# The first load of an RMSNorm-GELU kernel, split by rows over both DMA queues, with two of the last stores merged

## Chip, cores, metric

One core of one Trainium2 chip. The metric is the device time of one execution in microseconds, median of several runs; the profile's span is some 1.8 us shorter, because it starts and ends inside the execution.

## The reference

```python
# x: (8, 1024, 2048) float32, gamma: (2048,), eps: 1e-5
rms = np.sqrt(np.mean(x ** 2, axis=-1, keepdims=True) + eps)
out = gamma * x / rms
return 0.5 * out * (1 + np.tanh(np.sqrt(2 / np.pi) * (out + 0.044715 * out ** 3)))
```

8,192 rows of 8 KB are read once and written once: 67.1 MB each way.

## The kernel before

The rows are cut into 16 groups. A group is 128 partitions of 4 rows each (32 KB in one piece per partition, 4 MB in all), and six slots in SBUF hold groups. SyncE issues the loads, ScalarE issues gamma and the stores, each on its own DMA queue (q1 is SyncE's, q10 is ScalarE's). Per group, ScalarE squares and sums four rows, GpSimd makes 1/rms, VectorE multiplies by gamma (which TensorE has spread over the partitions in PSUM), ScalarE does Gelu and issues the store. A slot is loaded again when its store has landed.

```python
P = 128; ROWS = 4; SLOTS = 6; NARROW = 128
# ...
whole = [(R, [(0, R * D)])]
store_pieces = {
    0: [(R, [(0, NARROW), (NARROW, R * D)])],
    G - 1: [(1, [(r * D, r * D + D)]) for r in range(R)],
}
def load(g):
    nc.sync.dma_start(out=slot[g % SLOTS], in_=x3[g])
# ... squares, scale, inverse_rms cut ...
def gelu_store(g):
    # ... per entry (n, stores): Gelu on n rows, then
            for a, b in stores:
                nc.scalar.dma_start(out=dst[:, a:b], in_=flat[:, a:b])

for k in range(0, D, CHUNK):                      # four gamma pieces of 2 KB
    nc.scalar.dma_start(out=gamma_row[...], in_=gamma[k : k + CHUNK]...)
for g in range(SLOTS):
    load(g)
# ... memsets, warm-up, the matmuls that spread gamma ...
for g in range(G + 1):
    if g < G:
        squares(g); inverse_rms(g); scale(g)
    if g:
        gelu_store(g - 1)
        if g - 1 + SLOTS < G:
            load(g - 1 + SLOTS)
```

Of the kernel before, what the change touches and what calls it, by code (L numbers as in the profile page):

```python
# [1 line left out]

# [4 lines left out]

FP32 = mybir.dt.float32
ALU = mybir.AluOpType
ACT = mybir.ActivationFunctionType  # L10

P = 128
ROWS = 4
SLOTS = 6

GW = 32
CHUNK = 512

NARROW = 128


@with_exitstack
def kernel(
    ctx: ExitStack,
    tc: tile.TileContext,
    x: bass.AP,
    gamma: bass.AP,
    eps: bass.AP,
    out: bass.AP,
):  # L30




    nc = tc.nc
    D = x.shape[-1]
    R = ROWS
    eps_f = float(eps)
    x3 = x.rearrange("b s d -> (b s) d").rearrange("(g p r) d -> g p r d", p=P, r=R)
    o3 = out.rearrange("b s d -> (b s) d").rearrange("(g p r) d -> g p r d", p=P, r=R)  # L40
    G = x3.shape[0]

    sbuf = ctx.enter_context(tc.tile_pool(name="sbuf", bufs=1))
    psum = ctx.enter_context(
        tc.tile_pool(name="psum", bufs=1, space=bass.MemoryType.PSUM)
    )
    slot = [sbuf.tile([P, R, D], FP32, name=f"slot{i}") for i in range(SLOTS)]
    gamma_row = sbuf.tile([1, D // GW, GW + 4], FP32, name="gamma_row")
    ones = sbuf.tile([1, P], FP32, name="ones")
    warm = sbuf.tile([1, 1], FP32, name="warm")  # L50
    power = sbuf.tile([P, R], FP32, name="power")
    ssq = sbuf.tile([P, G, R], FP32, name="ssq")
    rstd = sbuf.tile([P, G, R], FP32, name="rstd")
    ms = sbuf.tile([P, R], FP32, name="ms")
    y = sbuf.tile([P, R], FP32, name="y")
    z = sbuf.tile([P, R], FP32, name="z")
    gamma_ps = psum.tile([P, D], FP32, name="gamma_ps")
    junk = psum.tile([P, D], FP32, name="junk")


    whole = [(R, [(0, R * D)])]
    store_pieces = {
        0: [(R, [(0, NARROW), (NARROW, R * D)])],
        G - 1: [(1, [(r * D, r * D + D)]) for r in range(R)],
    }
    scale_pieces = {G - 1: [(0, 1), (1, 1), (2, 1), (3, 1)]}

    def load(g):
        nc.sync.dma_start(out=slot[g % SLOTS], in_=x3[g])  # L69

    def squares(g):
        for r in range(R):
            nc.scalar.activation(  # L73
                out=junk,
                in_=slot[g % SLOTS][:, r, :],
                func=ACT.Square,
                accum_out=ssq[:, g, r : r + 1],
            )

    def scale(g):  # L80
        for r, n in scale_pieces.get(g, [(0, R)]):
            rows = slot[g % SLOTS][:, r : r + n, :]
            nc.vector.tensor_tensor(  # L83
                out=rows,
                in0=rows,
                in1=gamma_ps.unsqueeze(1).to_broadcast([P, n, D]),
                op=ALU.mult,
            )

    def inverse_rms(g):  # L90

        v = nc.gpsimd
        v.tensor_scalar(  # L93
            out=ms, in0=ssq[:, g, :], scalar1=1.0 / D, scalar2=eps_f,
            op0=ALU.mult, op1=ALU.add,
        )
        v.tensor_tensor(out=y, in0=ms, in1=power, op=ALU.pow)  # L97
        v.tensor_tensor(out=z, in0=y, in1=y, op=ALU.mult)  # L98
        v.tensor_tensor(out=z, in0=z, in1=ms, op=ALU.mult)  # L99
        v.tensor_scalar(  # L100
            out=z, in0=z, scalar1=-0.5, scalar2=1.5, op0=ALU.mult, op1=ALU.add
        )
        v.tensor_tensor(out=rstd[:, g, :], in0=z, in1=y, op=ALU.mult)  # L103

    def gelu_store(g):
        flat = slot[g % SLOTS].rearrange("p r d -> p (r d)")
        dst = o3[g].rearrange("p r d -> p (r d)")
        row = 0
        for n, stores in store_pieces.get(g, whole):
            for r in range(row, row + n):  # L110
                nc.scalar.activation(  # L111
                    out=slot[g % SLOTS][:, r, :],
                    in_=slot[g % SLOTS][:, r, :],
                    func=ACT.Gelu_apprx_tanh,
                    scale=rstd[:, g, r : r + 1],
                )
            row += n
            for a, b in stores:
                nc.scalar.dma_start(out=dst[:, a:b], in_=flat[:, a:b])  # L119

    with tc.manual_schedule():
        for k in range(0, D, CHUNK):
            nc.scalar.dma_start(
                out=gamma_row[:, k // GW : (k + CHUNK) // GW, 0:GW],
                in_=gamma[k : k + CHUNK].rearrange("(o a b) -> o a b", o=1, b=GW),
            )
        for g in range(SLOTS):
            load(g)
        nc.gpsimd.memset(power, -0.5)  # L129
        nc.vector.memset(warm, 0.0)  # L130
        nc.vector.memset(ones, 1.0)  # L131
        nc.scalar.activation(out=warm, in_=warm, func=ACT.Gelu_apprx_tanh)  # L132
        for k in range(0, D, CHUNK):
            nc.tensor.matmul(  # L134
                out=gamma_ps[:, k : k + CHUNK],
                lhsT=ones,
                rhs=gamma_row[:, k // GW : (k + CHUNK) // GW, 0:GW],
                start=True,
                stop=True,
            )  # L140
        for g in range(G + 1):
            if g < G:
                squares(g)
                inverse_rms(g)
                scale(g)
# [6 lines that stand above are left out]
# [1 line left out]
_INS = ['x', 'gamma', 'eps']  # L153
_OUTS = [((8, 1024, 2048), 'float32')]

_NUMBERS = {'eps': 9.999999747378752e-06}


# [26 lines left out]
```

## Time and profile before

| | before |
|---|---|
| time | 317.27 us (317.25 to 317.39, 4 runs) |
| span | 315.5 us |
| ScalarE, VectorE busy | 80%, 44% |
| DMA engines, both queues | 99.1% of 16 engines' span |
| mean rate | 426 GB/s |

From the table of DMA issues (count, size of one, median us from issue to landing):

```profile
slot<-in_x_dram SPq DMA_DIRECT2D x16, 4096.0 KB, 29.9
out_dram<-slot ACTq DMA_DIRECT2D x14, 4096.0 KB, 43.3
gamma_row<-in_gamma_dram ACTq DMA_DIRECT2D x4, 2.0 KB, 10.3
```

A 4 MB transfer alone would take about 10 us (4.19 MB at 430 GB/s). That loads take 30 us and stores 43 us from issue to landing says that both queues are long: the transfers are what everything else waits for.

The end of the chain of waits (start, length, what):

```profile
242.11 29.47 DMA slot<-in_x_dram
271.61 2.01 ACT junk L73 x2
...
287.31 0.34 ACTq L119
```

The last load lands at 271.6 us. From there to the end of the span, 44 us, only stores move, and ScalarE finishes the last group beside them by 297 us.

### The profile page before, as it was taken

To read this page: it belongs to the slowest core of one execution; us is meant where nothing else is said; L and a number is where in the kernel's file an instruction comes from. 1 tells how busy PE (TensorE), PEld (TensorE's weight loads), DVE (VectorE), ACT (ScalarE), POOL (GpSimd) and SP (SyncE) were. 2 spreads that over 40 slices of the span, in tenths; PEclk is the share of its full clock that TensorE was granted. 3 is DMA by queue.
4 is the path that set the end of the run, shared out by engine and by line. 5 is a ranking of instruction groups with operands and counts; after the bars stand their busy time and mean duration, and the time that the engine had idled before them with its cause. 6 is when DMAs were issued, how large, how long until landed. Compare 5 with 4: busy or idle time off the path is not lost.

```text
span 315.5 us, 479 instructions
## 1 busy us (share of the span) xinstructions
PE 7.9 (3%) x8; PEld 2.1 (1%) x8; DVE 139.4 (44%) x21; ACT 251.2 (80%) x194; POOL 32.3 (10%) x101
## 2 busy tenths in 40 slices
PE   0810000000000000000000000000000000000000
PEld 0200000000000000000000000000000000000000
DVE  0028909091918282827328082370824609480000
ACT  1289999999999999989596895969959599598500
POOL 0020202020202020202020020200202002020000
DMA  8999999999999999999999999999999999999997
GB/s 329 404 461 403 459 413 396 453 406 462 403 461 407 457 407 458 411 453 416 449 428 440 432 432 432 432 440 424 446 416 453 411 453 411 453 415 449 416 418 314
DMA packets 5315, 134.25 MB, mean 426 GB/s; under 512 B 704, under 2 KB 832, under 8 KB 832
## 3 DMA queue, kind: packets, MB, share of 16 engines
q1 hardware_dynamic: 2304, 67.11, 49.7%
q10 hardware_dynamic: 3008, 67.12, 49.4%
q14 instruction: 3, 0.02, 0.0%
HBM read 67.12 MB, written 67.11 MB: 425 GB/s over the span
## 4 chain that ended last, share of the span: by engine, by line
ACT 38%; DMA 32%; another core or an unknown queue 18%; issue 5%; ACTq 1%; SPq 0%
ACT slot L111 21%; DMA slot<-in_x_dram 16%; ACT junk L73 16%; DMA out_dram<-slot 15%; ACTq L119 1%; SPq L69 0%; ACTq L111 0%; ACTq L73 0%
## 5 line engine op out<-in xcount | busy, mean ns | idle before, releaser
L83 DVE TENSOR_TENSOR slot<-slot,gamma_ps 128x8192 f32<-128x8192 f32 (+1 forms) x19 | 139.2, 7338 | 142.3 <-ACT junk L73 142.3
L73 ACT ACTIVATE junk<-slot 128x2048 f32<-128x2048 f32 x64 | 120.4, 1881 | 40.8 <-DMA slot<-in_x_dram 36.8
L111 ACT ACTIVATE slot<-slot,rstd 128x2048 f32<-128x2048 f32 x64 | 123.0, 1987 | 1.7 <-ACT slot L111 1.7
L93 POOL TENSOR_SCALAR ms<-ssq 128x4 f32<-128x4 f32 x16 | 3.1, 194 | 242.8 <-ACT junk L73 242.8
L97 POOL TENSOR_TENSOR y<-ms,power 128x4 f32<-128x4 f32 x16 | 16.1, 1009 | 1.3
L73 ACT ACTIVATION_READ_ACCUMULATOR junk<-slot 128x1 f32 x64 | 11.9, 186 | 0.0
L134 PE MATMUL gamma_ps<-gamma_row,ones 1*128 1x512 f32 x8 | 7.9, 1112 | 9.2 <-DMA gamma_row<-in_gamma_dram 9.2
L132 ACT ACT_TABLE_LOAD x1 | 1.3, 1283 | 3.3 <-issue 3.3
L99 POOL TENSOR_TENSOR z<-z,ms 128x4 f32<-128x4 f32 x16 | 3.2, 201 | 1.3
L103 POOL TENSOR_TENSOR rstd<-z,y 128x4 f32<-128x4 f32 x16 | 3.2, 200 | 1.3
L98 POOL TENSOR_TENSOR z<-y 128x4 f32<-128x4 f32 x16 | 3.2, 200 | 1.3
L100 POOL TENSOR_SCALAR z<-z 128x4 f32<-128x4 f32 x16 | 3.1, 195 | 1.4
L134 PEld LDWEIGHTS gamma_ps<-gamma_row,ones 1*128 1x128 f32 x8 | 2.1, 306 | 13.4 <-issue 8.7
L130 DVE MEMSET warm<- 1x1 f32 x1 | 0.1, 59 | 0.8 <-PEq L166 0.8
L132 ACT ACTIVATE warm<-warm 1x1 f32<-1x1 f32 x1 | 0.2, 203 | 0.0
L131 DVE MEMSET ones<- 1x128 f32 x1 | 0.2, 165 | 0.0
L129 POOL MEMSET power<- 128x4 f32 x1 | 0.1, 102 | 0.3 <-POOLq L166 0.3
L166 POOL MEMSET const-float32-0.0<- 128x1 f32 x1 | 0.1, 99 | 0.2 <-issue 0.2
L166 POOL MEMSET const-bfloat16-1.0<- 128x1 bf16 x1 | 0.1, 102 | 0.0
L166 POOL MEMSET const-uint8-127<- 128x1 uint8 x1 | 0.1, 102 | 0.0
L166 POOL MEMSET const-float32-1.0<- 128x1 f32 x1 | 0.1, 99 | 0.0
## 6 DMA issues: line engine op xcount, KB each, us to landing
slot<-in_x_dram SPq DMA_DIRECT2D x16, 4096.0 KB, 29.9
out_dram<-slot ACTq DMA_DIRECT2D x14, 4096.0 KB, 43.3
out_dram<-slot ACTq DMA_DIRECT2D x4, 1024.0 KB, 17.5
out_dram<-slot ACTq DMA_DIRECT2D x1, 4032.0 KB, 28.5
gamma_row<-in_gamma_dram ACTq DMA_DIRECT2D x4, 2.0 KB, 10.3
out_dram<-slot ACTq DMA_DIRECT2D x1, 64.0 KB, 14.4
```

The costliest lines, as they stand in the source:

```text
L73: nc.scalar.activation(out=junk, in_=slot[g % SLOTS][:, r, :], func=ACT.Square, accum_out=ssq[:, g, r : r + 1],)
L83: nc.vector.tensor_tensor(out=rows, in0=rows, in1=gamma_ps.unsqueeze(1).to_broadcast([P, n, D]), op=ALU.mult,)
L93: v.tensor_scalar(out=ms, in0=ssq[:, g, :], scalar1=1.0 / D, scalar2=eps_f, op0=ALU.mult, op1=ALU.add,)
L97: v.tensor_tensor(out=y, in0=ms, in1=power, op=ALU.pow)
L98: v.tensor_tensor(out=z, in0=y, in1=y, op=ALU.mult)
L99: v.tensor_tensor(out=z, in0=z, in1=ms, op=ALU.mult)
L100: v.tensor_scalar(out=z, in0=z, scalar1=-0.5, scalar2=1.5, op0=ALU.mult, op1=ALU.add)
L103: v.tensor_tensor(out=rstd[:, g, :], in0=z, in1=y, op=ALU.mult)
L111: nc.scalar.activation(out=slot[g % SLOTS][:, r, :], in_=slot[g % SLOTS][:, r, :], func=ACT.Gelu_apprx_tanh, scale=rstd[:, g, r : r + 1],)
L119: nc.scalar.dma_start(out=dst[:, a:b], in_=flat[:, a:b])
L132: nc.scalar.activation(out=warm, in_=warm, func=ACT.Gelu_apprx_tanh)
L134: nc.tensor.matmul(out=gamma_ps[:, k : k + CHUNK], lhsT=ones, rhs=gamma_row[:, k // GW : (k + CHUNK) // GW, 0:GW], start=True, stop=True,)
```

## The change

The intent: ScalarE stands idle until load 0 has landed. Half of its rows per partition now come over each queue, both issued at once. The diff also merges the stores of rows 0 and 1 of the last group into one.

```diff
-        G - 1: [(1, [(r * D, r * D + D)]) for r in range(R)],
+        G - 1: [(2, [(0, 2 * D)])] + [(1, [(r * D, r * D + D)]) for r in (2, 3)],
...
     with tc.manual_schedule():
+        nc.sync.dma_start(out=slot[0][:, 0 : R // 2], in_=x3[0, :, 0 : R // 2])
+        nc.scalar.dma_start(out=slot[0][:, R // 2 :], in_=x3[0, :, R // 2 :])
         for k in range(0, D, CHUNK):
             nc.scalar.dma_start(
... gamma as before ...
-        for g in range(SLOTS):
+        for g in range(1, SLOTS):
             load(g)
```

## The prediction

> **What bounds the kernel now.** I read the page first: engine shares, the DMA row, the queues. Then I cut the span into stretches, and last looked at the start, because the change is there.
>
> The page, kernel before (the third column of a queue line is its share of 16 DMA engines' span):
>
> ```profile
> PE 7.9 (3%) x8; PEld 2.1 (1%) x8; DVE 139.4 (44%) x21; ACT 251.2 (80%) x194; POOL 32.3 (10%) x101
> DMA  8999999999999999999999999999999999999997
> DMA packets 5315, 134.25 MB, mean 426 GB/s; under 512 B 704, under 2 KB 832, under 8 KB 832
> q1 hardware_dynamic: 2304, 67.11, 49.7%
> q10 hardware_dynamic: 3008, 67.12, 49.4%
> HBM read 67.12 MB, written 67.11 MB: 425 GB/s over the span
> ```
>
> The busiest compute engine, ScalarE, is at 80%. The DMA engines are at nine tenths or more in 38 of 40 slices, and the two queues' shares add up to 99.1% of all 16 engines for the whole span. So bytes bound this kernel: 67.1 MB in, 67.1 MB out, none of it removable. The packets of q1, the load queue: 16 loads of 128 rows of 32 KB are 2048, and 16 completions on each of 16 engines are the other 256, tiny ones. One 32 KB packet takes 0.497 x 16 x 315.5 / 2048 = 1.225 us on its engine, or 16 x 32,768 B / 1.225 us = 428 GB/s for all 16.
>
> The same by stretches (the last two columns are the DMA engines' mean busy share and GB/s):
>
> ```profile
> 1.50:6.00 4.50, 0.00 (x0) 0.00 (x0) 0.00 (x0) 1.49 (x2) 0.00 (x0) 1.00 0.97 350
> 6.00:14.00 8.00, 4.82 (x5) 1.49 (x6) 0.00 (x0) 0.53 (x1) 0.00 (x0) 1.00 1.07 456
> 14.00:30.00 16.00, 3.07 (x4) 0.61 (x2) 8.40 (x1) 14.33 (x15) 2.01 (x6) 1.00 0.99 428
> 30.00:50.00 20.00, 0.00 (x0) 0.00 (x0) 11.69 (x3) 19.49 (x16) 4.00 (x12) 1.00 1.01 421
> 132.00:272.00 140.00, 0.00 (x0) 0.00 (x0) 65.22 (x8) 112.70 (x87) 13.98 (x42) 1.00 1.00 432
> 300.00:312.00 12.00, 0.00 (x0) 0.00 (x0) 0.00 (x0) 0.00 (x0) 0.00 (x0) 1.00 0.97 412
> 312.00:314.00 2.00, 0.00 (x0) 0.00 (x0) 0.00 (x0) 0.00 (x0) 0.00 (x0) 1.00 0.70 295
> ```
>
> The reader is to see that the DMA share is about 1.00 from 1.5 us until 312 us. Loads alone (14 to 30 us) run at 428 GB/s, loads with stores (132 to 272) at 432: one queue already fills the engines. The only place where a full share moves few bytes is the first: 350 GB/s in 1.5 to 6 us, although the share is 0.97. By the packet records the first packet on each engine takes some 2 us and every later one 1.213. That costs 4.5 x (432 - 350) / 432 = 0.85 us. Between 30 and 50 us, 20 x 11 / 432 = 0.5 us is lost. Nothing moves before about 1.7 us and after about 314 us.
>
> The start in order of time, and two waits of SyncE's queue:
>
> ```profile
> 13.47 1.88 ACT L73 ACTIVATE junk<-slot 128x2048 f32<-128x2048 f32 x1 [8.70 <-DMA slot<-in_x_dram]
> 21.60 8.69 DVE L83 TENSOR_TENSOR slot<-slot,gamma_ps 128x8192 f32<-128x8192 f32 x1 [20.60 <-ACT junk L73]
> 23.06 1.88 ACT L73 ACTIVATE junk<-slot 128x2048 f32<-128x2048 f32 x1 [1.49 <-DMA slot<-in_x_dram]
> ```
>
> ```profile
> SPq L69 <- DMA out_dram<-slot: 224.3, 10, 53.7
> SPq L69 <- DMA gamma_row<-in_gamma_dram: 10.2, 2, 7.9
> ```
>
> ScalarE waits 8.70 us for the first load, the squares of group 0 end at 21.6, and it waits again, 1.49 us, for load 1. This is the idleness that the change aims at. But SyncE itself waits 224.3 us in all for stores to land before it may reuse a slot: compute is ahead of the transfers nearly everywhere.
>
> **What the Trainium skill says.** "DMA: Bandwidth & Descriptors", section "Issuing engines are not separate DMA queues", says that DMAs run on the same 16 DMA engines whichever engine issued them and that several issuers only save issue time. The trace agrees so far as it can: one queue alone gives 428 GB/s, two give 432. Section "Queues, rings and completion order" says that each DMA engine takes turns among its rings packet by packet. The packet records agree: in the start each tiny gamma packet lies between two 32 KB load packets, 1.21 us apart. "Specifications" of that page puts the fabric ceiling at 435 GB/s; 432 here is 99% of it. "Perfetto Trace Analysis", section "DMA Optimizations", says that splitting helps if DMA engines are generally idle; here they are not.
>
> **The change part by part.** (1) Load 0 becomes two DMAs with 16 KB per partition. Bytes are equal; packets go from 128 of 32 KB to 256 of 16 KB. The packet records have 309 ns for an 8 KB store packet and 1213 for 32 KB; a straight line through them has 7.7 ns per packet besides the bytes. So 128 more packets and 16 more completions of 9 ns cost (128 x 7.7 + 16 x 9) / 16 = 0.07 us.
>
> (2) The diff also merges the stores of rows 0 and 1 of the last group: 128 packets and 16 completions fewer, minus 0.07 us. It delays that first piece by one row of Gelu, about 2.4 us (289.80 to 292.22 in the chain of waits). But the last piece is issued at 297.05 and takes 17.6 us to land, and every earlier one takes 17.5: there is a store backlog of 17 us, so a piece 2.4 us later costs nothing. Sum of (1) and (2): zero.
>
> (3) When does load 0 land? It lands now 12.7 us after issue, with the engines busy all that time; the same 4.19 MB can't land sooner on the same engines. If both halves share turns from the start, both land near 12.5 us. If ScalarE's ring is seen later, as with gamma (issued at 0.72, first packets near 6.1 us), SyncE's half lands near 8 to 10 us, and the other half takes turns with the 32 KB packets of load 1: it would land at 14 to 17 us. The built program shows that the squares of rows 0 and 1 wait for SyncE's half alone, so ScalarE can start two rows early and then wait. Squares 0 end between 20.5 and 25 instead of 21.6.
>
> (4) The gamma pieces now queue behind a half load on ScalarE's ring. Each takes two turns of 1.21 us beside load packets, so four take up to 9.7 us more, and gamma lands at 20 to 27 us instead of 14.5 (landings now: 7.5 to 11.9 us after issue). With the matmuls some 2 us after, VectorE starts on group 0 between 22 and 29 us instead of 21.6, and the first large store, now issued at 38.77, comes 0 to 7 us later. That is off the path: the six loads alone are 25.2 MB, 58 us at 430 GB/s, so the engines have load packets until about 60 us without any store, and then stores that have been waiting.
>
> (5) The built program shows different semaphore reuse at SyncE: load 3 now waits for ScalarE's half, load 4 for load 1 (it waited for a gamma piece, the 10.2 us line). Load 3 then goes out near 13 to 17 us, load 4 near 23 us. At each moment at least one full load of 9.7 us still stands in the queue, so the ring doesn't run dry. The waits of later stores on earlier ones keep their pattern.
>
> Sum: +0.07 - 0.07, plus whatever the 0.85 us of the first packets becomes. I give two rings some chance to overlap part of it, -0.1 us on average. 317.28 - 0.1 is 317.2.
>
> **The rivals.** A, the intended one: ScalarE begins 3 to 5 us earlier and the whole kernel shifts by it, to about 313. For it speaks the 8.70 us wait; against it that compute is ahead already (224.3 us of SyncE's waits are for stores) and that the bytes would have to move at 134.25 MB / (313 - 1.8 - 1.7 - 1.4 us) = 436 GB/s, which no long stretch shows. B: the later gamma and first store open a gap in the transfers. It needs both rings empty; the first 60 us hold 58 us of loads alone, so it would cost at most 1 to 2 us: 318 to 319. C: the two small losses (0.85 and 0.5 us) both vanish, or a similar one is added where the rings meet: 316 or 318. D: the later first store shifts how loads and stores interleave. Since both kinds run at 428 to 432, a shift is worth under half a per cent.
>
> **Range and chances.** Not transferring: 1.7 us ahead, 1.4 behind, 1.8 outside the span; lost within: 0.85, 0.5, and the uneven end of 0.6. Even all of it but the part outside the span is 5.1 us, 1.6%, so a 2% gain is nearly excluded. A 2% loss needs 6.3 us with idle engines, for which I see no place. The three runs of before lie within 0.12 us. I take 317.2 us with 316.3 to 318.0 and the chances 0.01, 0.98, 0.01.
>
> **What would show it right or wrong.** Right: DMA row still nines, queue shares still adding to 99%, q1 about 2 MB lighter and q10 as much heavier, steady stretch at 432 GB/s; ScalarE's first squares earlier than 13.47 (if SyncE's half lands first) but the end moved by less than 1 us; gamma landing at 20 us or later and VectorE starting group 0 later. Step (3) is wrong if both halves land well before 12 us; (4) if gamma lands before 15 us. The whole is wrong if some slice after the first shows a DMA share below 9, or if the last load lands (now near 271.5) more than 1 us earlier or later and the end follows it.

## The result and the profile after

317.30 us (317.12 to 317.46, 4 runs) against 317.27 us: ratio 1.000, 95% interval 0.9983 to 1.0017. Here and below a ratio is the mean time of one kernel's fast runs over that of the other's fast runs of the same rounds, so it need not be quite the ratio of the medians.

The page of the changed kernel, the lines that answer to those of before:

```profile
DMA  7999999999999999999999999999999999999997
q10 hardware_dynamic: 3008, 69.22, 50.9%
q1 hardware_dynamic: 2304, 65.01, 48.2%
```

2.1 MB moved from q1 to q10. The shares again sum to 99.1%, and the DMA row is full from the second slice to the last but one. The stretches (last two columns: DMA share, GB/s):

```profile
1.50:6.00 4.50, 0.00 (x0) 0.00 (x0) 0.00 (x0) 1.49 (x2) 0.00 (x0) 1.00 0.96 350
...
132.00:272.00 140.00, 0.00 (x0) 0.00 (x0) 68.80 (x9) 117.88 (x91) 14.69 (x46) 1.00 1.00 432
```

The start moves 350 GB/s as before and the steady part 432 as before. Two rings fill the DMA engines no better than one.

What did move is the order of events at the start:

```profile
13.09 1.88 ACT L73 ACTIVATE junk<-slot 128x2048 f32<-128x2048 f32 x1 [7.86 <-DMA slot<-in_x_dram]
...
22.88 2.07 PE L136 MATMUL gamma_ps<-gamma_row,ones 1*128 1x512 f32 x2 [0.37 <-DMA gamma_row<-in_gamma_dram]
...
23.09 1.88 ACT L73 ACTIVATE junk<-slot 128x2048 f32<-128x2048 f32 x1 [1.89 <-DMA slot<-in_x_dram]
...
25.05 17.29 DVE L83 TENSOR_TENSOR slot<-slot,gamma_ps 128x8192 f32<-128x8192 f32 x2 [24.05 <-PE gamma_ps L136]
...
41.54 0.34 ACTq L119 DMA_DIRECT2D out_dram<-slot  x1
```

ScalarE starts 0.38 us earlier (13.09 against 13.47) and gives it back at once: it waits 1.89 us instead of 1.49 for load 1 and starts on it at 23.09 against 23.06. Gamma's last piece lands near 22.9 us, so VectorE starts on group 0 at 25.05 instead of 21.60, and the first large store goes out at 41.54 instead of 38.77 us: 2.8 us later. The landings of what was issued first:

```profile
slot<-in_x_dram ACTq DMA_DIRECT2D x1, 2048.0 KB, 12.5
slot<-in_x_dram SPq DMA_DIRECT2D x1, 2048.0 KB, 12.3
...
gamma_row<-in_gamma_dram ACTq DMA_DIRECT2D x4, 2.0 KB, 17.1
```

And at the end, the chain of waits of the changed kernel:

```profile
244.79 24.35 DMA slot<-in_x_dram
269.17 2.01 ACT junk L73 x2
```

The last load lands 2.4 us earlier than before (269.2 against 271.6), although the first store went out later. While the engines are full, bytes that one queue doesn't move, the other does: if the loads finish sooner, more stores are left for the end, and the sum is the same. How far the last load moves does not follow from the first store alone. In the runs below, the squares of the last group start at 271.3 us with the first large store 8.3 us later than before (gamma ahead of the half load), at 270.9 us with it 7.5 us later (compute later by 8.1 us), and at 275.9 us with it at the same 38.7 us (narrow piece dropped); all three medians are within 0.6 us of before's. What is shown is that the end does not follow the last load, not what moves the last load.

### The profile page after: what moved, and what is told of

The parts are those of the page before. It is cut to its first block, busy times and chain, and to the rows that moved or that the text cites. A ratio compares the mean times of both kernels' runs of the same rounds, so it can differ in the third digit from the quotient of the medians.

```text
span 315.7 us, 480 instructions
## 1 busy us (share of the span) xinstructions
PE 8.2 (3%) x8; PEld 2.0 (1%) x8; DVE 139.3 (44%) x21; ACT 251.2 (80%) x194; POOL 32.3 (10%) x101
## 2 busy tenths in 40 slices
DMA packets 5315, 134.25 MB, mean 425 GB/s; under 512 B 704, under 2 KB 832, under 8 KB 832
## 4 chain that ended last, share of the span: by engine, by line
ACT 35%; DMA 29%; another core or an unknown queue 18%; issue 5%; DVE 3%; ACTq 2%; PE 1%; SPq 0%; DVEq 0%
ACT slot L111 21%; DMA out_dram<-slot 15%; ACT junk L73 14%; DMA slot<-in_x_dram 8%; DMA gamma_row<-in_gamma_dram 6%; DVE slot L83 3%; ACTq L119 1%; PE gamma_ps L136 1%; ACTq L125 1%; SPq L69 0%; ACTq L123 0%; ACTq L111 0%; DVEq L83 0%
## 6 DMA issues: line engine op xcount, KB each, us to landing
slot<-in_x_dram ACTq DMA_DIRECT2D x1, 2048.0 KB, 12.5
slot<-in_x_dram SPq DMA_DIRECT2D x1, 2048.0 KB, 12.3
```

## The experiments

Eleven kernels ran, with three to five rounds each against the kernel before. All gave correct results.

| run | median us | ratio to before (95%) |
|---|---|---|
| load split alone | 317.59 | 1.0004 (0.9992 to 1.0017) |
| store merge alone | 317.43 | 1.0002 (0.9988 to 1.0015) |
| narrow first store dropped | 317.43 | 1.0001 (0.9989 to 1.0014) |
| compute and first store earlier | 318.15 | 1.0021 (1.0008 to 1.0033) |
| compute later by 8.1 us | 317.97 | 1.0016 (1.0001 to 1.0031) |
| compute later by 16.3 us | 319.05 | 1.0054 (1.0040 to 1.0068) |
| compute later by 24.4 us | 323.69 | 1.0202 (1.0188 to 1.0215) |
| gamma ahead of the half load | 317.68 | 1.0010 (0.9990 to 1.0029) |
| all loads halved | 333.54 | 1.0524 (1.0500 to 1.0548) |
| all full stores halved | 327.34 | 1.0313 (1.0255 to 1.0371) |
| loads and stores in 16 KB packets | 318.71 | 1.0036 (1.0021 to 1.0051) |

### The two parts alone

The load split alone is the changed kernel with the last group's stores as before; the merge alone is the other way round.

```diff
# load split alone, against the changed kernel
-        G - 1: [(2, [(0, 2 * D)])] + [(1, [(r * D, r * D + D)]) for r in (2, 3)],
+        G - 1: [(1, [(r * D, r * D + D)]) for r in range(R)],
# merge alone, against the kernel before: the same two lines the other way
```

> The first load split over both queues, the stores of the last group as before. My theory (16 DMA engines are the bound, so only bytes and packets count): 317.3 us, +0.07 us of packets, ratio 1.000 within 0.002. Rival A (the earlier first landing is on the path): about 0.4 us faster, the 13.47 to 13.09 us by which the first squares moved, with the store merge hiding it in the combined change. Rival B (later gamma is on the path): 2 to 3 us slower, the 38.77 to 41.54 us by which the first large store moved.

> Only the stores of rows 0 and 1 of the last group merged, nothing split. My theory: 317.2 us, -0.07 us of packets, ratio 1.000 within 0.002, because 17 us of store backlog lie behind the piece that goes out 2.4 us later. Rival (a later first piece of the last group delays the end): up to 2.4 us slower.

Both are the kernel before, within 0.2%. So the result isn't a gain of one part hidden by a loss of the other. The 0.07 us of packets for either part lie below what these intervals resolve. Rival A's 0.4 us would be a ratio of 0.9987, just outside the interval of the split; 2 us or more of rival B or of the merge's rival are excluded.

### Compute earlier: does the start of compute matter at all?

A harder test of the intent than the change itself. Load 0 goes out in four pieces of one row each, on SyncE alone, and Gelu and store of group 0 come ahead of the squares of group 1.

```diff
-        for g in range(SLOTS):
+        for r in range(R):
+            nc.sync.dma_start(out=slot[0][:, r], in_=x3[0, :, r])
+        for g in range(1, SLOTS):
             load(g)
...
+            if g == 0:
+                gelu_store(0)
             if g:
-                gelu_store(g - 1)
+                if g > 1:
+                    gelu_store(g - 1)
```

> Load 0 in four pieces of one row on SyncE, and Gelu and store of group 0 ahead of the squares of group 1, so that the first store goes out about 5 us earlier than 38.8. My theory: first squares near 6 us instead of 13.5, squares of group 0 done near 15 us instead of 21.6, first large store near 33 us, and the kernel still 317.3 us within 0.6. Rival A (compute's start is on the path): 4 to 6 us faster, 311 to 313 us.

The order of time in that run:

```profile
5.33 1.88 ACT L73 ACTIVATE junk<-slot 128x2048 f32<-128x2048 f32 x1 [0.52 <-DMA slot<-in_x_dram]
...
31.78 0.34 ACTq L119 DMA_DIRECT2D out_dram<-slot  x1
...
278.65 1.88 ACT L73 ACTIVATE junk<-slot 128x2048 f32<-128x2048 f32 x1 [3.66 <-DMA slot<-in_x_dram]
...
294.36 0.34 ACTq L119 DMA_DIRECT2D out_dram<-slot  x1
```

The first squares start 8.1 us earlier (5.33 against 13.47), the first large store goes out 7.0 us earlier, and the kernel is 0.2% slower, a little outside the 0.6 us that I had allowed. The last load lands 7.0 us later (squares of the last group at 278.65 against 271.61). The store of group 14 then goes out at 294.36 instead of 287.31, and that is too late: counted from the packet records, the DMA engines have nothing to move for 1.1 us between 294.0 and 296.0 us, where the kernel before has no gap. So the backlog of stores at the end, which hides the last group's compute, was used up. The profiled span is 1.0 us longer than before's (316.5 against 315.5): 1.1 us of gap, 0.45 us of longer or more packets (the mean time of all packets on an engine, summed from the trace's records, is 313.1 us against 312.7), and about 0.5 us back, because the engines end more evenly. The intended mechanism, an earlier start, has no value in this kernel; taken 7 us far, it opens a small hole at the other end.

### Compute later: how much slack is there?

The squares of group 0 are done once, twice or three times more before the real ones; the extra results are overwritten.

```diff
+        for _ in range(1):      # 1, 2, 3
+            squares(0)
         for g in range(G + 1):
```

> The squares of group 0 are done once more before the real ones, result thrown away and overwritten: 8.1 us more on ScalarE before anything else, first large store at about 46.9 us instead of 38.8. My theory: the six loads alone keep the DMA engines busy until about 60 us, so 317.3 us within 0.7. Rival A (compute's start on the path): 325.4 us.

> The same twice, 16.3 us more, first large store at about 55 us. My theory: still before the loads run out near 60 us, but store 1 goes out only near 71 us, about when store 0 has landed; 317.3 to 319.5 us, at most a gap of 2 us. Rival A: 333.6 us.

> The same three times, 24.4 us more, first large store at about 63 us. My theory: now the loads run out near 60 us before a store is there, the DMA row gets a gap there and small ones after it, and the kernel gets 3 to 9 us slower, 320 to 326 us. Rival A: 341.7 us. Rival D (stores and loads share without any effect of order, compute never matters): 317.3 us.

By the ratios, 8.1 us of work put ahead of everything cost 0.5 us, 16.3 us cost 1.7 us, 24.4 us cost 6.4 us. All three lie in the ranges of "loads keep the DMA engines busy until about 60 us", and none near those of "compute's start is on the path". In the third run the transfers do open a gap, where the loads have run out and stores come one at a time:

```profile
60.00:66.00 6.00, 0.00 (x0) 0.00 (x0) 3.42 (x1) 5.55 (x5) 0.00 (x0) 1.00 0.62 258
66.00:74.00 8.00, 0.00 (x0) 0.00 (x0) 2.84 (x1) 7.94 (x8) 2.00 (x6) 1.00 0.78 336
```

A DMA share of 0.62 and 0.78 over these 14 us is 6 x 0.38 + 8 x 0.22 = 4.0 us of idle engines. This view books a packet where it starts; counted by the packets' own starts and ends, the engines idle for 3.3 us here and for 1.5 us more from 74 to 84 us. With 2.2 us of longer packets (314.9 us per engine against 312.7) that makes up the 6.9 us by which this profiled span is longer. For the second run I had allowed a gap of up to 2 us, but what the first two paid isn't idleness: an engine idles 3.1 and 2.8 us in their whole span, 2.8 us in the kernel before. Over 1.213 us for 32 KB, the packets of the delay of 16 us took 3.12 us per engine in excess up to 90 us, those of the kernel before 1.41 us: a difference of 1.7 us, which is the loss; for the delay of 8 us the same sum is 1.91 us, 0.5 more, which is its loss. They are slow, 1.3 to 2.3 us, in clusters at the start and where a queue starts again. The changed kernel's first store, 2.8 us later, lies well inside this slack.

### The slow packets when the first store begins

Before, the load packets between 45 and 48 us took up to 2.0 us, after, those between 47 and 51 us up to 2.1 us: in sum 0.7 and 0.8 us too long per engine. In both this is when the narrow first piece of the first store (64 KB, 512 B per row) ends.

```diff
-        0: [(R, [(0, NARROW), (NARROW, R * D)])],
```

> The 64 KB piece of the first store, 512 bytes per row, is not cut off: one 4 MB store. In both traces the load packets run 1.3 to 2.1 us instead of 1.213 just when that narrow piece ends (45 to 48 us before, 47 to 50 us after), about 0.7 to 0.8 us per engine. If the narrow piece causes it: those packets stay at 1.21 us and the kernel takes 316.5 us, 0.7 us less. If the turn from loads alone to loads with stores causes it: the same loss when the first large store begins, and 317.3 us.

317.43 us, ratio 1.0001. Without the narrow piece, the load packets took up to 1.97 us between 39.9 and 42 us instead, just after the first store was issued, and the excess was again 0.7 us per engine. So the narrow piece does not cause it; it comes with the first store, whatever its shape. Why, I didn't find out.

### Gamma ahead of the half load

```diff
-        nc.scalar.dma_start(out=slot[0][:, R // 2 :], in_=x3[0, :, R // 2 :])
         for k in range(0, D, CHUNK):
             nc.scalar.dma_start(
... gamma ...
+        nc.scalar.dma_start(out=slot[0][:, R // 2 :], in_=x3[0, :, R // 2 :])
         for g in range(1, SLOTS):
```

> The changed kernel with one thing moved: ScalarE issues the four gamma pieces first and its half of load 0 after them. If gamma is late in the changed kernel because it stands behind a half load on ScalarE's ring: gamma has landed by 15 us again, VectorE starts on group 0 when the squares are done instead of at 25.05 us, and the first large store goes out near 38.8 us or at most as late as the second half makes it. My theory for the time: 317.3 us all the same, within 0.6, because neither landing is on the path. Rival B (later gamma ate a gain): 0.5 to 2 us faster than the changed kernel and the one before.

```profile
8.25 1.88 ACT L73 ACTIVATE junk<-slot 128x2048 f32<-128x2048 f32 x1 [2.85 <-DMA slot<-in_x_dram]
...
26.54 1.88 ACT L73 ACTIVATE junk<-slot 128x2048 f32<-128x2048 f32 x1 [14.26 <-DMA slot<-in_x_dram]
...
30.61 17.29 DVE L83 TENSOR_TENSOR slot<-slot,gamma_ps 128x8192 f32<-128x8192 f32 x2 [29.61 <-ACT junk L73]
```

Gamma was there early (median 7.0 us from issue), and VectorE waited for the squares as expected. But ScalarE's half load, issued 2.6 us after SyncE's, now met the 32 KB packets of load 1 and landed at 26.5 us, so VectorE started still later, at 30.61 us. The time is 1.001 of before, with runs from 317.2 to 318.8. Neither gamma nor the half load is on the path. The run also shows the case that the prediction had feared for the change: a half load whose ring is served later is landed last.

### Why not split every load?

If splitting load 0 is free, one may want to split all. Both halves go out on SyncE here.

```diff
-        nc.sync.dma_start(out=slot[g % SLOTS], in_=x3[g])
+        for r in (0, R // 2):
+            nc.sync.dma_start(
+                out=slot[g % SLOTS][:, r : r + R // 2], in_=x3[g, :, r : r + R // 2]
+            )
```

> Every load is cut by rows into two DMAs, both issued by SyncE. By the straight line through the packet durations each such load costs 0.07 us more, 16 of them 1.1 us: 318.4 us. If only bytes count: 317.3 us. If more DMAs in turn (waits for a free semaphore at SyncE) let the load ring run dry: over 319 us, and DMA share below 1.00 somewhere after the start.

333.54 us, 5.2% slower: the number fits the third branch, but the load ring did not run dry in the middle: load packets began in every 2 us up to 290 us. The profile shows a gap near the end (columns as before):

```profile
295.00:300.00 5.00, 0.00 (x0) 0.00 (x0) 0.00 (x0) 0.40 (x1) 0.00 (x0) 1.00 0.81 347
300.00:305.00 5.00, 0.00 (x0) 0.00 (x0) 3.36 (x2) 4.97 (x5) 1.19 (x2) 1.00 0.09 39
305.00:310.00 5.00, 0.00 (x0) 0.00 (x0) 1.13 (x1) 5.00 (x4) 0.81 (x5) 1.00 0.00 0
```

For over 10 us next to nothing moves: the last load landed only near 299 us (271 before), nearly all stores had drained by then, and the compute of the last group lies bare. That is not the whole loss. Of the 17.7 us by which this profiled span is longer than before's (333.2 against 315.5), 11.2 us are idle engines, and 6.5 us are packets (319.2 us per engine against 312.7), where 1.1 us was expected for the further ones; the others were slower, and why is open. The table of DMA issues says how it came to this:

```profile
slot<-in_x_dram SPq DMA_DIRECT2D x32, 2048.0 KB, 46.8
out_dram<-slot ACTq DMA_DIRECT2D x14, 4096.0 KB, 19.4
```

Stores landed in 19.4 us instead of 43.3, and half loads took 46.8 us where whole ones took 29.9. With turns taken packet by packet, a load packet of 16 KB and a store packet of 32 KB per round give the loads a third of the bytes. The packet records agree: from 144 to 156 us, with both queues at work, 99 load packets (1.62 MB) and 101 store packets (3.31 MB) began. That was a new theory, formed after this run, and two kernels tested it. The first halves the stores instead:

```diff
-    whole = [(R, [(0, R * D)])]
+    whole = [(R, [(0, R * D // 2), (R * D // 2, R * D)])]
```

> The mirror of the run that halved all loads and took 333.5 us: now every full store is cut by rows into two DMAs of 16 KB packets, the loads stay whole at 32 KB. If the DMA engines take turns packet by packet, so that the smaller packets get the smaller share of bytes: the loads now get two thirds where both queues have work, the last load lands earlier than 271 us or waits on slots only, no gap at the end, and the cost is the packets alone, about 1 to 2 us: 318.3 to 319.5 us. If the 16 us came from more DMAs in turn and their semaphores, or from 16 KB packets as such: about 330 us or more here too.

327.34 us (325.3 to 329.2), far over the 318.3 to 319.5 that I expected and nearer to the other branch, "about 330 us or more". The shares did turn round:

```profile
slot<-in_x_dram SPq DMA_DIRECT2D x16, 4096.0 KB, 20.9
out_dram<-slot ACTq DMA_DIRECT2D x28, 2048.0 KB, 36.5
...
320.00:322.00 2.00, 0.00 (x0) 0.00 (x0) 0.00 (x0) 0.00 (x0) 0.00 (x0) 1.00 0.06 25
```

Loads land in 20.9 us instead of 29.9 (the first two lines). But from 319 to 324 us the DMA share is 0.05 to 0.08 (the last line is one such stretch): one engine of sixteen, 1/16 = 0.06, finishes alone, some 4 us after the last of the others. And the packets summed to 317.1 us per engine instead of 312.7, 1.0 us of it the further packets, the rest slow ones, mostly where a queue starts again. So turning the inequality round did not make it harmless, and the rival, that more DMAs in turn cost the time, is not excluded by this run.

The second makes both directions 16 KB without a further DMA: each slot is padded by 64 B after 16 KB, so a partition's 32 KB are no longer one piece in SBUF.

```diff
-    slot = [sbuf.tile([P, R, D], FP32, name=f"slot{i}") for i in range(SLOTS)]
+    H = R // 2
+    slot = [sbuf.tile([P, 2, H * D + 16], FP32, name=f"slot{i}") for i in range(SLOTS)]
...
-        nc.sync.dma_start(out=slot[g % SLOTS], in_=x3[g])
+        nc.sync.dma_start(
+            out=slot[g % SLOTS][:, :, 0 : H * D],
+            in_=x3[g].rearrange("p (a b) d -> p a (b d)", a=2),
+        )
... stores alike, compute on the same rows, narrow piece dropped ...
```

> As many DMAs and semaphores as the kernel before, but each slot's row is padded in SBUF after 16 KB, so that loads and full stores both go in 16 KB packets (the narrow piece of the first store is dropped, which made no difference). If turns by packet decide: equal packets give equal shares again, the last load lands near 272 us as in the kernel before, and only 4,000 more packets of 7.7 ns on 16 engines are paid, about 2 us: 319 to 320 us. If 16 KB load packets as such are slow: 330 us or more.

318.71 us, 1.15 us over before's runs (ratio 1.0036), a little under the 319 to 320 us expected.

```profile
slot<-in_x_dram SPq DMA_DIRECT2D x16, 4096.0 KB, 36.8
out_dram<-slot ACTq DMA_DIRECT2D x15, 4096.0 KB, 37.1
```

Equal packets give equal landings, 36.8 and 37.1 us, and the last load lands at 275.6 us. So 16 KB packets as such cost a third of a per cent. The halved kernels cost 3 to 5%, but they differ from this one in two things: unequal packets, and two DMAs for one. The landings and the packet counts show that the packets' sizes set the shares of the queues; what the rest of the cost comes from is not shown, because no kernel had unequal packets without more DMAs, or more DMAs with equal packets. The completion records of the trace add a reason that I had not thought of. Each DMA engine completes its share of a load by itself, and a load counts as landed when the slowest has. From the first to the last of the 16 completions of the last load:

```text
before              1.7 us
changed             1.6 us
all loads halved   14.8 us   (0.4 to 0.6 us in the first seven, then growing unevenly)
all stores halved   2.7 us
16 KB both          1.3 us
```

With the loads halved, the engines drift apart, and of the 28 us by which the last load is late some 13 are this wider spread (14.8 against 1.7). What sets off the drift, and why one engine alone lagged with the stores halved, stays open.

This concerns the change only so far: it makes unequal packets only during load 0, when the other queue carries gamma and load 1 and no store, and only for 2 MB.

## Why the prediction was right, point by point

- **The bound.** Right. The queue shares sum to 99.1% in both kernels and the steady stretch is at 432 GB/s in both; doing compute 8 us earlier or later moved the time by less than 0.25%.
- **Parts (1) and (2), packets and the merged store.** Right as far as can be seen: 1.0004 and 1.0002. The 7.7 ns per packet got a test at scale in the padded kernel, 9,139 packets against 5,315: 3,824 x 7.7 ns / 16 = 1.8 us estimated. Its packet records summed to 314.6 us per engine against 312.7, which is 1.9 more; the time rose by 1.15 us only, so some 0.7 us came back elsewhere.
- **Part (3), the landing of load 0.** The first of its two cases came true: halves shared turns from the start and landed 12.3 and 12.5 us after issue. The second case was seen when the half load was issued 2.6 us later behind gamma, and there the prediction's 14 to 17 us was too early: eight 16 KB packets per engine, in turn with 32 KB ones, took from 12.1 to 25.9 us. From the 6.1 us that the prediction assumed, that would have been near 20 us, an estimate from these 13.8 us.
- **Part (4), gamma and the first store.** Right: gamma's four pieces completed 2.43 us apart, two turns of 1.21 us each, and the last had landed at 22.9 us (20 to 27 predicted), VectorE started at 25.05 (22 to 29), the first large store went out 2.8 us later (0 to 7). It cost nothing, and the delayed kernels show the slack that absorbs it.
- **Part (5), semaphores.** SyncE waited 20.6 us in two waits for loads where it had waited 10.2 us for gamma, as derived from the built program, and the queue did not run dry.
- **The -0.1 us for overlap of the first packets.** Wrong in mechanism, though too small to see: the first stretch moved 350 GB/s in both, so two rings hid nothing of it. The reading beside it, that every packet after the first took 1.213 us, was not quite right either: 24 load packets between 45 and 49 us took 1.3 to 2.0 us.
- **The sign to watch for.** The last load did land more than 1 us earlier, 2.4 us, but the end did not follow it. The prediction had named the two together; the runs separate them: over the kernels within 0.3% of before, the squares of the last group start anywhere from 269.2 to 278.7 us.
- **Rivals.** A is refuted by the kernel with the earlier start, B by the kernels with the delayed one at this size. C's small losses neither vanished nor grew. D holds for a shift in time; but the interleaving of loads and stores is not harmless in general: it cost 3 to 5% in the two kernels where one side's DMAs were halved.

## What to carry to other kernels

When the DMA engines are full from the first microsecond to the last, an earlier first landing was worth nothing here: look whether a wait ends with more bytes moved, not whether it gets shorter. Check both ends of such a kernel: what stores don't take at the start they take at the end, and the backlog there is what hides the last group's compute. If two queues work at once, look at the sizes of their packets (the contiguous piece per partition), because they set each queue's share; here, cutting the DMAs of one side alone cost 3 to 5%, far more than the further packets, and the same packet size on both sides without further DMAs cost 0.4%.

## What the Trainium skill lacked or had wrong

- "DMA: Bandwidth & Descriptors", "Queues, rings and completion order": that an engine takes turns by packet agrees with these traces, but the page does not draw the consequence. With 16 KB load and 32 KB store packets, loads took 46.8 us to land and stores 19.4; with equal ones 36.8 and 37.1. The first kernel was 5.2% slower; it also had two DMAs per load, and how much of the loss each of the two makes is not separated.
- The same page, "Bandwidth", asks for DMAs of 1 MiB or more for three quarters of the peak. The halved kernels keep to it and reach it (2 and 4 MB, 403 and 413 GB/s), and are still 5.2% and 3.1% slower than with 4 MB on both sides: the size of one DMA is not the whole rule. That the packets of the two queues against each other belong to it is likely, not shown.
- No page gives a size for how far the DMA engines can drift apart over many DMAs issued from SyncE and ScalarE: 14.8 us between the first and last engine's completion of one load, against 1.7 us in the kernel before.
- No page tells of the slow packets when a queue starts: 1.3 to 2.3 us instead of 1.213 for 32 KB, some 0.7 us per engine at the start of the kernel and again at the first store.
